# A smaller DMA scratch, and its SBUF given to more buffers in the mixers of a streaming encoder step

## The chip, the core and the metric

The kernel runs on one core of one Trainium2 chip. A core has five engines that run their own instruction queues in order and meet only at semaphores: TensorE (PE, matrix products, with its weight loads shown as PEld), VectorE (DVE), ScalarE (ACT), GpSimd (POOL) and SyncE (SP), which here only issues DMAs. ACT and POOL issue DMAs too. A DMA is issued in the order of the queue that it stands in, and an issue that has to wait holds back all that is behind it on that queue. On-chip memory (SBUF) has 128 partitions; a buffer takes some bytes of each. PE writes its results to another memory, PSUM, from which ACT and DVE fetch them.

The metric is the device time of one launch in microseconds (us), median of several runs. A profile is one execution, and its span runs from the first to the last instruction of the program.

## The reference

One layer of an encoder is applied to a prompt (2048 rows of 1024) and to a sample (8 requests of 16 rows) that shares the weights and brings a cache. Cut to what matters:

```python
h = rms_norm(x, norm_g[0])
z = h @ w_in                                   # columns: qa ka va | qb kb vb ob | ib fb
att = band_attention(qa, ka, va)               # 8 heads x 64, own chunk of 64 and 8 before, bias by distance
                                               # sample: 512 cached keys and values, and its own 16
hb, (c1, n1, m1) = mlstm_sequence(qh, kh, vh, ig, lf, c0, n0, m0)   # 4 heads x 128, a matrix state
mix = concat(rms_norm(att), sigmoid(ob) * head_norm(hb)) @ w_out
x = x + rms_norm(mix, norm_g[1])
u = rms_norm(x, norm_g[2]) @ w_up              # 1024 -> 5632
y = causal_conv_width_3(u)
x = x + rms_norm((gelu(gate) * up) @ w_down, norm_g[3])             # 2816 -> 1024
```

It returns the new rows, the keys and values to keep, the mLSTM's states, and the last rows of `u`. The sample's mLSTM starts from states that are inputs: for each of 4 heads and 8 requests a 128x128 matrix with a vector beside it (`state_c`, 129 columns).

## The kernel before, in words

All values are float32. A product is made of three products of "high" and "low" parts: each operand is split by ACT (a copy to a rounded type, the high part) and DVE (what is left, the low part), and `mm3` (lines 93 to 97) issues high*high, high*low, low*high. So every weight that comes from memory goes through a raw float32 tile, a split by ACT and DVE, and two tiles that PE reads.

The work up to about 1300 us, the mixers:

- *Projection.* The 17 tiles of 128 rows (16 of the prompt and the sample's one) are taken in two halves, `HALVES`. `norm_tile` (L209) loads a tile of x (`xr`), norms it and turns it on PE (`hT`). For each half 14 groups of columns of `w_in` are gone through, `GROUPS`: `va`, `qk`, `qb`, `vo`. `load_group` (L1158) brings a group's weights in two halves of 1056 columns at most through the tile `wraw` (the DMA at L1169, splits at L1175 and L1176). The results leave PSUM through a stage tile of two buffers (`st`), and go to DRAM by DMAs that ACT issues (L239, L275).
- *Attention.* `load_head` (L321) brings queries, keys and values of a head and a quarter of the prompt back from DRAM in raw tiles (`raw_tile`, L282), splits them (L342 to L356), and `att_unit` (L364) makes scores, weights and output. The bias depends on the distance alone: `build_bias` (L291) writes it to DRAM once for each head and row, eight broadcasts `relrow` (L302), from which `nb` is loaded (L325). `attention_sample` does the same for the sample, with keys and values of the cache in raw tiles (L847, L897).
- *mLSTM.* `prep_prompt` and `prep_sample` make the stabilisers; `mlstm` goes over pairs of blocks of 128 rows, with a result tile `num` of two buffers; `mlstm_sample` (L726) handles a head of the sample, and its `batches` takes two requests at a time: it loads their states into `cs` (L769), multiplies (L781, L782), updates the states in place (L785, L786) and stores them from there (L787). Before the change `cs` shares the two buffers of `num`.
- *Output projection.* `w_out_steps` (L929) brings `w_out` through `wraw` too; `project` (L962) makes the mix for one tile after another and writes the result to DRAM (`x2d`).

Two streams of units, attention and mLSTM, are interleaved with the projection by hand-written costs (`pump`, L171). That fixes the program's order. The tile framework then schedules it: it simulates the program on its own timeline and fixes each engine's order of instructions and each tile's buffer, waits included. So how many buffers a tile has changes where instructions stand on every engine. Priorities at a few places are pinned (`keep_in_program_order`).

From L1262 on comes the feed-forward part, in three blocks of rows: the up projection by a seven-product scheme (`product`, L1411), the convolution (L1428 on, with POOL's small copies), and the down projection (`down`). Its pools take the SBUF of the mixers' pools once those are closed (`open_ffn`, L1037). The only DMAs that POOL issues are 24 stores of finished rows in this part (L1378).

[...]

Of the kernel before, what the change touches and what calls it, by code (L numbers as in the profile page):

```python
# [10 lines left out]
F32 = mybir.dt.float32  # L11
# [6 lines left out]
P = 128  # L18
D = 1024
# [10 lines left out]
LS = 512 + DS  # L30
# [14 lines left out]
def hymba_step(ctx: ExitStack, tc: tile.TileContext, I: dict, O: dict):  # L45
    nc = tc.nc
# [13 lines left out]
    def ps_sm(name):  # L60
        return psum.tile([P, 512], F32, tag="sm", name=name)
# [25 lines left out]
    def norm_row(i):  # L87
        t = const.tile([P, D], F32, tag="grow", name=f"norm_row{i}")
        nc.sync.dma_start(t, I["norm_g"][i:i + 1, :].broadcast_to([P, D]))
        return t  # L90
# [35 lines left out]
    pr = p1.enter_context(tc.tile_pool(name="pr", bufs=1))  # L126
    pa = p1.enter_context(tc.tile_pool(name="pa", bufs=2))
    pm = p1.enter_context(tc.tile_pool(name="pm", bufs=2))
# [151 lines left out]
    relrow = dt_([HA, P, SQ], "relrow")  # L280

    def raw_tile(name):  # L282
        return pa.tile([P, LS], F32, tag="raw", name=name, bufs=3)

    rel = []

    def load_bias():
        rel.append(raw_tile("reln")[:HA, :SQ - 383])
        tc.keep_in_program_order(nc.sync.dma_start(rel[0], I["rel_rev"][:, 0:SQ - 383]))

    def build_bias():  # L291
        ext = dt_([HA, SQ], "ext")

        def unit():
            far, near = raw_tile("relf")[:HA, :383], rel[0]
            nc.vector.tensor_scalar(near, near, -1.0, None, op0=ALU.mult)
            nc.vector.tensor_copy(far, near[:, 0:1].broadcast_to([HA, 383]))
            nc.sync.dma_start(ext[:, 383:SQ], near)
            nc.sync.dma_start(ext[:, 0:383], far)
            yield 0.0, 0.75  # L300
            for h in range(HA):
                tc.keep_in_program_order(nc.sync.dma_start(relrow[h], ext[h:h + 1, :].broadcast_to([P, SQ])))  # L302
                yield 0.0, 0.0
                if h % 2:
                    yield 0.0, 0.0

        yield unit()
        yield FLUSH
# [12 lines left out]
    def load_head(s):  # L321
# [7 lines left out]
        s.nb = nbs[hh]  # L329
        rows = slice(hh * 64, hh * 64 + 64)  # L330
        qr = raw_tile(f"qraw{nm}")[:, :512]
        krs = [raw_tile(f"kraw{nm}_{g}")[:, :512] for g in s.segs]
        for r in range(2):
# [392 lines left out]
    def mlstm_sample(h):  # L726
        md, dec, cols = stab["s"]
        e = DH + 1
        nm = f"s{h}"
        col = lambda i: cols[:, i, h:h + 1]  # L730
        s = SimpleNamespace()
# [33 lines left out]
        def batches(bp):  # L765
            yield 0.0, 0.0
            bs = slice(2 * bp, 2 * bp + 2)
            cs = pm.tile([P, 2, e], F32, tag="num", name=f"cs{h}_{bp}", bufs=2)
            nc.sync.dma_start(cs, I["state_c"][h][:, bs])  # L769
            qz = pm.tile([P, 2, P], F32, tag="mqk", name=f"qz{h}_{bp}", bufs=2)  # L770
            nc.gpsimd.memset(qz, 0.0)
            for i in range(2):
                c = slice((2 * bp + i) * DS, (2 * bp + i + 1) * DS)
                nc.gpsimd.tensor_copy(qz[:, i, c], s.qt[:, c])
            vz = pm.tile([P, 2, e], F32, tag="mvo", name=f"vz{h}_{bp}", bufs=2)
            nc.vector.tensor_tensor(vz, s.va.unsqueeze(1).broadcast_to([P, 2, e]),
                                    ind[:, bs].unsqueeze(2).broadcast_to([P, 2, e]), op=ALU.mult)
            yield 0.0, 0.3
            cu = ps_sm(f"cu{nm}_{bp}")
            for i in range(2):  # L780
                nc.tensor.matmul(cu[:, 2 * e:3 * e], qz[:, i, :], cs[:, i, :], start=(i == 0), stop=(i == 1))  # L781
            nc.tensor.matmul(cu[:, :2 * e], s.kw, vz.rearrange("p b e -> p (b e)"), start=True, stop=True)  # L782
            nc.vector.scalar_tensor_tensor(s.num[:, 0, :], cu[:, 2 * e:3 * e], col(1), s.num[:, 0, :],
                                           op0=ALU.mult, op1=ALU.add)
            nc.vector.tensor_tensor(cs, cs, dec[:, h, bs].unsqueeze(2).broadcast_to([P, 2, e]), op=ALU.mult)  # L785
            nc.vector.tensor_tensor(cs, cs, cu[:, :2 * e].rearrange("p (b e) -> p b e", b=2), op=ALU.add)  # L786
            nc.sync.dma_start(O["c_sample"][h][:, bs], cs)  # L787
            yield 0.85, 0.8
# [11 lines left out]
        for bp in range(DB // 2):  # L800
            yield batches(bp)
# [127 lines left out]
    def w_out_steps():  # L929

        big = []
        g1.append(norm_row(1))
        late = wpool.tile([P, 2112], F32, tag="wl", name="wor67", bufs=2)
        nc.sync.dma_start(late[:, :2 * D], I["w_out"][:, 6 * D:])
        for k in range(KT):
            if k < 6:
                raw = pr.tile([P, 1056], F32, tag="wraw", name=f"wor{k}")[:, :D]
                nc.sync.dma_start(raw, I["w_out"][:, k * D:(k + 1) * D])
                if k == 0:
                    yield 0.0, 0.0  # L940
            else:
                raw = late[:, (k - 6) * D:(k - 5) * D]
            if k % 3 == 0:
                big.append(phT.tile([P, 6, D], F32R, tag="hT", name=f"wo{k}", bufs=3))
            h_, l_ = big[-1][:, k % 3 * 2, :], big[-1][:, k % 3 * 2 + 1, :]
            for c in (slice(0, 512), slice(512, D)):
                if k < 4:
                    nc.scalar.activation(h_[:, c], raw[:, c], AF.Copy, scale=gatt[:, k:k + 1])
                    nc.vector.scalar_tensor_tensor(l_[:, c], raw[:, c], gatt[:, k:k + 1], h_[:, c],
                                                   op0=ALU.mult, op1=ALU.subtract)  # L950
                else:
                    nc.scalar.copy(h_[:, c], raw[:, c])
                    nc.vector.tensor_tensor(l_[:, c], raw[:, c], h_[:, c], op=ALU.subtract)
                if k < 6:
                    yield 0.0, 0.6
            wo.append((h_, l_))
# [201 lines left out]
    def load_group(gi):  # L1158

        i = SRC[GROUPS[gi]]  # L1160
        src, n = (I["w_in0"], 2112) if i == 0 else (I["w_in1"][i - 1], 2048)
        h = wpool.tile([P, 2112], F32R, tag="wh", name=f"wi{i}_h{gi}", bufs=2)
        l = wpool.tile([P, 2112], F32R, tag="wl", name=f"wi{i}_l{gi}", bufs=2)

        def steps():
            q = n // 2
            for s in range(2):
                raw = pr.tile([P, 1056], F32, tag="wraw", name=f"wi{i}_raw{s}")
                nc.sync.dma_start(raw[:, :q], src[:, s * q:(s + 1) * q])  # L1169
                yield 0.0, 0.0  # L1170
                yield 0.0, 0.0
                for e in range(2):
                    c = slice(s * q + e * q // 2, s * q + (e + 1) * q // 2)
                    r = raw[:, e * q // 2:(e + 1) * q // 2]
                    nc.scalar.copy(h[:, c], r)  # L1175
                    nc.vector.tensor_tensor(l[:, c], r, h[:, c], op=ALU.subtract)  # L1176
                    yield 0.0, 0.6

        return h, l, steps()
# [21 lines left out]
    for n_, (half, gi) in enumerate(seq):  # L1201
        wh, wl, _ = pend
# [5 lines left out]
        i = int(g[2])  # L1208
# [15 lines left out]
        if n_ == len(seq) - 1:  # L1224
            out = project([0, 1, 2, 3, 4, 5, 6, 7, SAMPLE, 8, 9, 10, 11, 12, 13, 14, 15])
            split = w_out_steps()
            next(split)
            next(out)
# [174 lines left out]
    for b, tiles in enumerate(FBLOCKS):  # L1403
# [74 lines left out]
        for f in range(NF):  # L1478
# [7 lines left out]
            e, c = ec[:, 0:512], ec[:, 512:1024]  # L1486
# [208 lines left out]
```

## Time and profile before

| | |
|---|---|
| time, median of 3 runs | 2796.26 us (2793.03 to 2800.73) |
| span of the profiled execution | 2784.7 us |
| mean granted TensorE clock | 0.998 |
| busy in the span | PE 98%, weight loads 92%, DVE 67%, ACT 51%, POOL 16% |
| DMA | 486.05 MB, 175 GB/s over the span |

The profiled execution has no time of its own beside its span; the median of the runs lies 11.6 us above the span, for what stands before the first and after the last instruction.

How to read the lines shown below. A line of the windows gives a stretch in us from the span's start, its length, and the busy time and number of instructions of each engine in it. A line of the waits says which engine, at which tile and line, waited for whom: microseconds in all, times, and the longest. A line of the timeline gives a start, a duration, engine, line, operation and tile, and in brackets the idle time of the engine before it and what ended it; "SPq" and "ACTq" are DMA issues, which count as no busy time. Names stand without buffer numbers: `cus` is the product of the sample's state, `qk_st` the stage of a projected group.

### The profile page before, as it was taken

The page shows a single profiled execution, that of the slowest core. Times are in us where ns is not written, and L with a number is a line of the kernel's source. Part 1 is how long each engine was busy: PE and PEld are TensorE (multiplying, and loading weights), DVE is VectorE, ACT ScalarE, POOL GpSimd, SP SyncE. Part 2 cuts the span into 40 slices and gives each one's busy share as a digit, 9 for nine tenths or more (in the row PEclk, how much of TensorE's full clock was granted, in tenths as well). Part 3 has the DMA queues.
Part 4 walks back from the last instruction along what each step waited for, and adds up shares of the span by engine and source line. Part 5 has one row for each costly group of instructions (what it writes and reads, how often), then busy time and mean ns, then how long its engine had stood idle before and what let it go on. Part 6 is the DMA issues. An engine that isn't in the chain of part 4 may idle for free.

```text
span 2784.7 us, 47088 instructions
## 1 busy us (share of the span) xinstructions
PE 2723.8 (98%) x16587; PEld 2548.3 (92%) x16587; DVE 1876.3 (67%) x3447; ACT 1409.1 (51%) x2836; POOL 437.4 (16%) x895
## 2 busy tenths in 40 slices
PE   8999999999999999999999999999999999999998
PEld 7899999998899998888999988899999878999887
DVE  5344455656556668666999986457877864888855
ACT  4355555644356666544454555345455543555543
POOL 1000010212000003244111110011111310222220
PEclk9999999999999999999999999999999999999999
DMA  5544355557555555356655455644544774555585
GB/s 185 155 119 136 103 174 162 164 157 217 162 173 148 144 179 171 107 176 227 187 172 167 167 176 174 219 142 153 160 152 141 276 263 152 172 179 180 192 309 190
DMA packets 311883, 486.05 MB, mean 175 GB/s; under 512 B 55426, under 2 KB 150622, under 8 KB 311518
## 3 DMA queue, kind: packets, MB, share of 16 engines
q1 hardware_dynamic: 271134, 442.92, 50.1%
q10 hardware_dynamic: 38592, 33.83, 3.6%
q0 software_dynamic: 1920, 6.29, 0.6%
q8 instruction: 130, 2.13, 0.3%
q14 instruction: 107, 0.88, 0.1%
HBM read 359.36 MB, written 126.70 MB: 175 GB/s over the span
## 4 chain that ended last, share of the span: by engine, by line
PE 55%; DVE 2%; DMA 1%; issue 1%; ACT 1%; POOL 1%; SPq 0%; DVEq 0%; POOLq 0%; ACTq 0%
PE uec L95 6%; PE uec L96 6%; PE uec L97 6%; PE dn L97 4%; PE dn L96 4%; PE dn L95 4%; PE ua L97 3%; PE ua L95 3%; PE ua L96 3%; PE dnm L97 2%; PE dnm L95 2%; PE dnm L96 2%; PE wo L97 2%; PE wo L95 2%; PE wo L96 2%; PE ub L96 1%
## 5 line engine op out<-in xcount | busy, mean ns | idle before, releaser
L95 PE MATMUL uec<-B,wuh 128*128 128x384 f32 (+1 forms) x720 | 234.9, 328 | 2.2 <-DVE uu L1419 1.1
L96 PE MATMUL uec<-B,wuh 128*128 128x384 f32 (+1 forms) x720 | 235.1, 327 | 0.0
L97 PE MATMUL uec<-B,wul 128*128 128x384 f32 (+1 forms) x720 | 233.9, 327 | 0.0
L1266 DVE TENSOR_TENSOR gl<-gr,gh 128x768 fp32r<-128x768 f32 (+3 forms) x141 | 120.4, 863 | 145.8 <-ACT gh L1265 144.5
L1265 ACT CAST gh<-gr 128x768 fp32r<-128x768 f32 (+3 forms) x141 | 102.0, 735 | 200.1 <-PE dn L96 183.2
L1265 ACT CAST wuh<-wu 128x512 fp32r<-128x512 f32 x255 | 141.7, 617 | 112.1 <-PE uec L96 103.2
L95 PE MATMUL dn<-wdh,gh 128*128 128x512 f32 x466 | 182.4, 391 | 2.3 <-DVE ug L1419 2.3
L96 PE MATMUL dn<-wdl,gh 128*128 128x512 f32 x466 | 183.4, 394 | 0.0
L97 PE MATMUL dn<-wdh,gl 128*128 128x512 f32 x466 | 167.9, 396 | 0.0
L1266 DVE TENSOR_TENSOR wul<-wu,wuh 128x512 fp32r<-128x512 f32 x255 | 164.6, 683 | 2.8 <-DMA x2d<-mx 2.8
L393 DVE CUSTOM_DVE_ANT_0 tmp<-s,nb 128x640 f32<-128x640 f32 (+4 forms) x128 | 94.4, 737 | 96.6 <-PE s L383 94.8
L95 PE MATMUL vo<-wi_h,hT 128*128 128x256 f32 x544 | 155.1, 285 | 0.6 <-DVE mt L199 0.6
L97 PE MATMUL vo<-wi_h,hT 128*128 128x256 f32 x544 | 155.6, 286 | 0.0
L96 PE MATMUL vo<-wi_l,hT 128*128 128x256 f32 x544 | 154.8, 285 | 0.0
L95 PEld LDWEIGHTS uec<-B,wuh 128*128 128x128 f32 x720 | 135.0, 188 | 4.2 <-DVE uu L1419 1.6
L95 PE MATMUL qk<-hT,wi_h 128*128 128x384 f32 (+1 forms) x384 | 128.7, 335 | 7.4 <-ACT qk_st L224 6.6
L96 PEld LDWEIGHTS uec<-B,wuh 128*128 128x128 f32 x720 | 135.2, 188 | 0.2
L97 PEld LDWEIGHTS uec<-B,wul 128*128 128x128 f32 x720 | 135.1, 188 | 0.0
L406 DVE TENSOR_TENSOR ptl<-pt,pth 128x640 fp32r<-128x640 f32 (+4 forms) x128 | 93.6, 737 | 57.1 <-ACT pth L405 56.0
L394 ACT ACTIVATE tmp<-tmp,mn 128x640 f32<-128x640 f32 (+4 forms) x128 | 97.6, 762 | 64.6 <-DVE mn L393 61.9
L96 PE MATMUL qb<-hT,wi_h 128*128 128x384 f32 (+1 forms) x384 | 127.8, 333 | 0.0
L96 PE MATMUL qk<-hT,wi_h 128*128 128x384 f32 (+1 forms) x384 | 127.6, 332 | 0.0
(412 smaller groups left out, 8873.0 us busy)
## 6 DMA issues: line engine op xcount, KB each, us to landing
wu<-in_w_up SPq DMA_DIRECT2D x220, 256.0 KB, 4.1
wu<-wsd SPq DMA_DIRECT2D x176, 256.0 KB, 4.2
wdr<-in_w_down SPq DMA_DIRECT2D x132, 256.0 KB, 5.6
gr<-gd SPq DMA_DIRECT2D x78, 384.0 KB, 3.6
wi_raw<-in_w_in SPq DMA_DIRECT2D x52, 512.0 KB, 4.0
wsd<-ws SPq DMA_DIRECT2D x88, 256.0 KB, 2.8
gd<-g SPq DMA_DIRECT2D x44, 384.0 KB, 3.5
kraw<-kTd SPq DMA_DIRECT2D x112, 128.0 KB, 3.2
```

Of the source, the lines that this page charges most:

```text
L95: nc.tensor.matmul(out, ah, bh, start=start, stop=False, skip_group_check=onto)
L96: nc.tensor.matmul(out, ah, bl, start=False, stop=False, skip_group_check=onto)
L97: nc.tensor.matmul(out, al, bh, start=False, stop=stop, skip_group_check=onto)
L393: nc.vector.tensor_tensor_reduce(o_, s_, b_, 1.0, 3e38, ALU.add, ALU.min, accum_out=mn)
L394: nc.scalar.activation(tmp[:, :n], tmp[:, :n], AF.Exp, bias=mn, scale=-1.0, accum_out=rsum[:, i % 4, hh:hh + 1])
L406: nc.vector.tensor_tensor(s.ptl[:, sl, qc], ptv, s.pth[:, sl, qc], op=ALU.subtract)
L1265: nc.scalar.copy(h, r)
L1266: nc.vector.tensor_tensor(l, r, h, op=ALU.subtract)
```

## The change

The scratch for POOL's DMAs is built with 4,096 bytes of a partition in place of 16,384. Of the 12,288 bytes, 10,512 are given out: a second buffer of `wraw` (4,224 bytes), two more of the raw attention tiles (2 x 2,112), and two buffers of its own for the sample state `cs` (2 x 1,032). Nothing is computed in another way; the number of instructions that compute and of DMAs is the same.

```diff
     def raw_tile(name):
-        return pa.tile([P, LS], F32, tag="raw", name=name, bufs=3)
+        return pa.tile([P, LS], F32, tag="raw", name=name, bufs=5)
...
         def batches(bp):
             yield 0.0, 0.0
             bs = slice(2 * bp, 2 * bp + 2)
-            cs = pm.tile([P, 2, e], F32, tag="num", name=f"cs{h}_{bp}", bufs=2)
+            cs = pm.tile([P, 2, e], F32, tag="cs", name=f"cs{h}_{bp}", bufs=2)
...
-                raw = pr.tile([P, 1056], F32, tag="wraw", name=f"wor{k}")[:, :D]
+                raw = pr.tile([P, 1056], F32, tag="wraw", name=f"wor{k}", bufs=2)[:, :D]
...
-                raw = pr.tile([P, 1056], F32, tag="wraw", name=f"wi{i}_raw{s}")
+                raw = pr.tile([P, 1056], F32, tag="wraw", name=f"wi{i}_raw{s}", bufs=2)
...
-    nc = bacc.Bacc("TRN2", target_bir_lowering=False, num_devices=1)
+    nc = bacc.Bacc("TRN2", target_bir_lowering=False, num_devices=1, dynamic_dma_scratch_size=4096)
```

## The prediction

> **What bounds the kernel now.** I read the head of the page first, then busy time by stage, then what PE waited for.
>
> ```profile
> span 2784.7 us, 47088 instructions
> PE 2723.8 (98%) x16587; PEld 2548.3 (92%) x16587; DVE 1876.3 (67%) x3447; ACT 1409.1 (51%) x2836; POOL 437.4 (16%) x895
> ```
>
> PE is busy for 2723.8 of 2784.7 us. The change takes no matmul away, so only the 60.9 us in which PE stood idle can be won. Where they lie is told by the view of windows (columns after the length: busy PE, weight loads, DVE, ACT, POOL, clock, DMA share, GB/s):
>
> ```profile
> 0.00:150.00 150.00, 129.66 (x888) 124.99 (x889) 67.45 (x168) 63.39 (x133) 12.07 (x40) 0.99 0.54 165
> 150.00:500.00 350.00, 349.35 (x2480) 344.37 (x2479) 178.76 (x408) 181.42 (x425) 17.72 (x58) 1.00 0.46 138
> 500.00:750.00 250.00, 237.14 (x1676) 223.97 (x1675) 144.75 (x413) 117.27 (x303) 46.02 (x132) 1.00 0.59 179
> 750.00:1000.00 250.00, 249.81 (x1891) 246.25 (x1890) 148.93 (x338) 149.23 (x357) 15.58 (x47) 1.00 0.54 159
> 1000.00:1300.00 300.00, 293.24 (x1720) 252.86 (x1719) 217.01 (x364) 158.92 (x382) 98.49 (x139) 1.00 0.50 161
> 1300.00:2784.70 1484.70, 1464.64 (x7943) 1355.91 (x7941) 1119.42 (x1757) 738.86 (x1239) 247.48 (x479) 1.00 0.57 189
> ```
>
> Idle PE is 20.3 us in the start, 12.9 us between 500 and 750, 6.8 us between 1000 and 1300, and 20.1 us in the feed-forward part, half of that its tail. The mixers proper (150 to 500, 750 to 1000) lose under 1 us. The view of waits names what ended the idle time (us in all, times, longest):
>
> ```profile
> PE qk L95 <- ACT qk_st L224: 6.6, 2, 3.3
> PE cus L781 <- DMA cs<-in_state_c: 5.0, 6, 2.0
> PE va L95 <- ACT hT L198: 3.0, 2, 1.9
> PE cus L781 <- DVE nums L783: 1.2, 1, 1.2
> ```
>
> Two of these lines, `qk_st` and `cs`, touch the buffers of the change. The 5.0 us for `cs` do so openly. The 6.6 us for `qk_st` do so through SP's queue.
>
> **The feed-forward part.** The built order of the changed kernel is the same, instruction for instruction on every engine, from the middle of the output projection (about 1260 us) to the end. Its term is 0; what can move lies before 1300 us.
>
> **Second raw weight buffer.** Now each half of a weight group waits until the half before it has been split. SP pays for that, and whatever stands behind the load in its queue:
>
> ```profile
> SPq L1169 <- DVE lg_s_s L515: 18.0, 1, 18.0
> ```
> ```profile
> 58.10 0.33 SPq L1169 DMA_DIRECT2D wi_raw<-in_w_in  x1
> 58.53 2.51 SPq L302 DMA_DIRECT2D relrow<-ext  x4
> 66.18 0.88 SPq L325 DMA_DIRECT2D nb<-relrow  x2
> 67.58 2.20 SPq L302 DMA_DIRECT2D relrow<-ext  x2
> 69.88 0.75 SPq L334 DMA_DIRECT2D qraw<-qTd  x1
> 96.78 1.16 SPq L302 DMA_DIRECT2D relrow<-ext  x2
> ```
> ```profile
> 62.19 1.12 ACTq L239 DMA_DIRECT2D qTd<-qk_st  x2
> 81.98 0.62 ACT L342 CAST qs<-qraw 128x512 fp32r<-128x512 f32 x1 [10.99 <-DMA qraw<-qTd]
> 82.50 0.47 ACT L224 COPY qk_st<-qk 128x384 f32<-128x384 f32 x1
> 98.68 1.13 ACTq L239 DMA_DIRECT2D qTd<-qk_st  x2
> 108.02 0.48 ACT L224 COPY qk_st<-qk 128x384 f32<-128x384 f32 x1 [7.30 <-DMA qTd<-qk_st]
> ```
>
> Read it as a chain. The sixth weight load waits 18.0 us, until 58.10. Behind it stand the broadcasts that lay out the attention bias (`relrow`); four take from 58.53 to 66.18, 7.65 us, before the first use of their result is issued. The query load comes behind two more of them; ACT stands 10.99 us in `qs` until 81.98, and the eviction behind it comes at 82.50: PE's first 3.3 us. The last two broadcasts at 96.78 run beside the query store of 98.68, so the next eviction waits 7.30 us for its stage: the second 3.3 us.
>
> With two buffers the sixth load waits for the split of the fourth half alone. In the changed order that split stands on DVE right behind the third tile's low part, near 22 us by my estimate (the third load goes out at 18.27 us today, in a row below, and no longer waits for its forerunner). So the first four broadcasts leave near 22 us instead of 58.53, and only two stand before the first queries. At half of 7.65 us they are through some 4 us after their issue, the query store of 62.19 is no longer late, and I expect `qs` near 70 us, while the eviction behind it is needed when PE finishes two more chunks, near 74. The first wait goes: -3.3 us (bounds -3.3 and 0). The last two broadcasts still follow the second stabiliser load (`dec`) and still meet a query store, but a few microseconds earlier, when the stage buffers are less behind: between 0 and -3.3 us, I take -2.0. Next in line is the cast of the first keys on ACT, which I put just ahead of PE's need.
>
> At the very start both halves of the first group are now fetched at once:
>
> ```profile
> 10.70 0.33 SPq L1169 DMA_DIRECT2D wi_raw<-in_w_in  x1
> 18.27 0.36 SPq L1169 DMA_DIRECT2D wi_raw<-in_w_in  x1
> 18.72 6.05 SPq L212 DMA_DIRECT2D xr<-in_x_prompt  x2
> 36.39 0.33 SPq L212 DMA_DIRECT2D xr<-in_x_sample  x1
> ```
>
> The half of 10.70 us moves in front of the second tile of x. That lets the first tile's matmuls run through, but the second tile lands about 2 us later, and the eighth tile (the second of the two from 18.72) falls behind the early broadcasts and the first bias load. From 22 plus 7.65 us it would be issued near 30 and land near 34, 2 to 3 us before PE asks for it. Gain and loss are of one size; I take 0, with bounds from -3.0 (the whole wait of `va` on `hT`) to +3.3 (one stall such as PE now has).
>
> **The sample state's own buffers.** The row of 5.0 us counts six waits. In one head, SP's rows (the first pair elsewhere, undisturbed; the second disturbed) and PE's:
>
> ```profile
> 443.34 0.34 SPq L787 DMA_DIRECT2D out_c_sample<-cs  x1
> 445.70 0.33 SPq L769 DMA_DIRECT2D cs<-in_state_c  x1
> ...
> 562.45 0.35 SPq L1169 DMA_DIRECT2D wi_raw<-in_w_in  x1
> 563.13 0.34 SPq L787 DMA_DIRECT2D out_c_sample<-cs  x1
> 567.91 0.33 SPq L769 DMA_DIRECT2D cs<-in_state_c  x1
> ```
> ```profile
> 441.99 0.60 PE L782 MATMUL cus<-vz,kws 128*128 128x258 f32 x2
> ...
> 570.12 0.68 PE L781 MATMUL cus<-cs,qz 128*128 128x129 f32 x4 [0.44 <-DMA cs<-in_state_c]
> ```
>
> A batch pair's buffer comes free when its state has been stored: 441.99 to 443.34 (1.35 us) until the store is issued, 2.36 us to the next load, and 570.12 - 567.91 = 2.21 us until PE has the data, 5.9 us together. Where a weight load of 512 KB went out just ahead, 562.45, the middle part is 4.78 us. With buffers of their own the first two loads of each head no longer wait for the mLSTM's `num` to be stored; in the changed order they stand far ahead. The third and fourth still wait for their own store. There 44 to 62 matmuls lie between the last product of a pair and the first of the pair after next; at 250 us / 1676 of the window 500 to 750, 0.149 us each, that is 6.6 to 9.2 us against 5.9. And no weight load stands between the first stores and loads of a head any more. I take -4.0 of the 5.0 + 1.2 us; bounds -6.2 and 0.
>
> [...]
>
> **Two more raw attention buffers.** No wait of PE names `qraw`, `kraw`, `vraw`, `skr` or `svr`; SP stands for them, and PE's idle share of the mixers proper is under 1 us. Term 0; if the cover goes it costs what SP's other heads of queue cost (below).
>
> **Smaller scratch.** [...]
>
> ```profile
> q0 software_dynamic: 1920, 6.29, 0.6%
> out_y_prompt<-f POOLq DMA_DIRECT2D x24, 256.0 KB, 5.5
> ```
>
> 24 issues in the whole program, 80 packets each, two close together at most. Term 0; a blocked POOL could add at most one landing of 5.5 us per issue, on an engine that is busy 16%.
>
> **What the new order moves.** The build reorders nearly all mixer work. Between about 380 and 700 us the attention and mLSTM matmuls stand some 10 us of PE work earlier; near the end of the mixers they stand some 10 us later, so that the last head's work falls among the projection of tiles 7 and 16. There DVE is busy 217.01 of 300 us (72%): 10 us of moved work bring up to 7.2 us of DVE work to a stretch that PE may wait on. The number of PE instructions that have under 3 us of other PE work between their cause and themselves is much the same in both orders, though (46 before, 52 after). I take 0, bounds -3.0 and +7.2.
>
> **Sum.** -3.3 - 2.0 + 0 - 4.0 + 0 = -9.3 us. The profiled span becomes 2775.4 us. The runs' median, 2796.26 us, is 11.6 us above the span; that remainder stays, so 2796.26 - 9.3 = 2787.0 us. A step of 0.3% is 8.4 us, about what a measurement of this kernel tells from none (the three runs spread over 7.7 us).
>
> **Rivals.**
>
> *More than that goes.* With all bounds on the good side, -3.3 - 3.3 - 3.0 - 6.2 - 3.0 = -18.8: 2777 us. For it speaks that each stall shifts everything behind it; against it, that six steps must all come out well.
>
> *The waits only move.* The broadcasts cost their 7.65 us of DMA wherever they run. Brought forward to 22 us they meet the loads of the x tiles, in the one stretch where PE has nothing else to do, and the `cs` loads put ahead meet them too. Then about 3.3 us return at the start and the second `qk_st` wait stays (+2.0), and two of the `cs` waits stay (+2): -9.3 + 7.3 = -2, 2794 us. [...]
>
> *Slower: SP's head of queue.* The changed order puts a store of `cs` and the load that waits for it back to back, twice per head, ahead of the sample's keys and values and the mLSTM loads:
>
> ```profile
> SPq L769 <- DMA out_c_sample<-cs: 22.8, 7, 4.4
> ```
>
> SP already stands 22.8 us in seven such waits. If the four of the last two heads, beside the sample attention, each held PE up for the longest of them, 4.4 us, that is +17.6: -9.3 + 17.6 = +8.3, 2804.6 us. It decides from two such holds on (-9.3 + 8.8, no gain), and at four the kernel is slower; against it, five raw buffers let the keys run ahead.
>
> *The change does not do what it says.* The extra buffers are not taken up because the order is fixed elsewhere; 2796 us. Against it, the built order does differ.
>
> **How the numbers follow.** The forecast (-14 to -4 us, 2782 to 2792) has 0.50, of which 0.34 lies beyond 0.3%; the larger gain 0.10; waits only moved 0.20; SP's queue 0.15; nothing or a blocked POOL 0.05. Faster by over 0.3%: 0.34 + 0.10 = 0.44. Slower: 0.15 + 0.03 = 0.18. Within: 0.38. The range leaves out half of the larger gain and the worse part of the slower case: 2774 to 2806 us.
>
> **What would show it.** Right: four `relrow` issues before 35 us; no `qk <- qk_st` wait of 3 us near 80; `cs` waits of PE under 1.5 us in all; idle PE between 500 and 750 near 9 us; the feed-forward part as long as before to 1 us. Wrong: `hT_pt` or `va` waits grown by over 3 us before 50; new PE waits on `skh`, `svh` or `ms` between 500 and 750; over 10 us idle between 1000 and 1300; POOL waiting at its DMAs.

## The result and the profile after

The changed kernel takes 2806.94 us (median of 4, 2803.42 to 2808.86), the kernel before 2795.14 us beside it. The ratio is 1.0041, 95% interval 1.0029 to 1.0053: 11.8 us slower, where 2787.0 us and a gain of 9.3 us were forecast. 2806.94 us lies above the range too.

The head of the page and the stretches of the windows, as shown of before:

```profile
span 2801.7 us, 47030 instructions
PE 2730.9 (97%) x16587; PEld 2552.3 (91%) x16587; DVE 1868.5 (67%) x3447; ACT 1403.6 (50%) x2836; POOL 436.3 (16%) x895
```
```profile
0.00:150.00 150.00, 128.98 (x871) 123.20 (x872) 67.62 (x167) 61.32 (x131) 14.11 (x40) 0.99 0.56 174
150.00:500.00 350.00, 347.06 (x2452) 341.20 (x2451) 174.91 (x410) 176.63 (x422) 14.32 (x56) 1.00 0.46 138
500.00:750.00 250.00, 239.08 (x1707) 227.77 (x1706) 144.61 (x414) 119.74 (x308) 45.21 (x138) 1.00 0.60 179
750.00:1000.00 250.00, 248.53 (x1868) 244.52 (x1867) 141.57 (x324) 143.36 (x346) 11.42 (x39) 1.00 0.52 151
1000.00:1300.00 300.00, 282.88 (x1660) 243.72 (x1659) 205.06 (x365) 158.10 (x381) 90.70 (x132) 0.98 0.47 151
1300.00:2801.70 1501.70, 1484.35 (x8038) 1371.89 (x8037) 1134.70 (x1772) 744.43 (x1253) 260.57 (x491) 1.00 0.57 189
```

PE idles 70.8 us in place of 60.9. By stretch (length minus busy PE): 21.0 at the start (20.3 before), 2.9 (0.7), 10.9 (12.9), 1.5 (0.2), 17.1 (6.8), and 17.4 (20.1) in the feed-forward part. The one that stands out is 1000 to 1300 us, where the clock fell to 0.98 as well. Idle time is not all of it: of the 17.0 us by which the two spans differ, 9.9 are idle and 7.1 are PE's busy time, for the same 16587 products (the last section comes back to this). All of it lies ahead of the feed-forward part, whose first product starts 19.8 us later (1333.3 us, 1313.5 before). The waits of PE:

```profile
PE hT_pt L67 <- DVE xr L219: 10.7, 4, 8.2
PE mT_pt L67 <- DVE mr L985: 9.3, 4, 6.1
PE va L95 <- ACT hT L198: 4.9, 4, 1.9
...
PE cus L781 <- DMA cs<-in_state_c: 2.2, 2, 1.3
PE h2T_pt L1093 <- DVE t L1119: 2.1, 1, 2.1
...
PE va L95 <- ACT qk_st L224: 1.7, 1, 1.7
```

The waits that the forecast rested on did shrink: `cs` from 5.0 + 1.2 to 2.2 us, the two waits of 3.3 us on `qk_st` to 1.7 + 0.5. In their place stand waits that the kernel before did not have, above all `mT_pt` on `mr`, 9.3 us, in the output projection. The order of the work there belongs to a step that the prediction had priced at nothing, "what the new order moves".

**The start.** SP's queue, and the ACT row for the first query:

```profile
1.72 0.91 SPq L1169 DMA_DIRECT2D wi_raw<-in_w_in  x2
...
11.21 0.80 SPq L769 DMA_DIRECT2D cs<-in_state_c  x2
...
24.58 0.33 SPq L1169 DMA_DIRECT2D wi_raw<-in_w_in  x1
25.00 3.15 SPq L302 DMA_DIRECT2D relrow<-ext  x4
...
43.60 0.33 SPq L212 DMA_DIRECT2D xr<-in_x_sample  x1
```
```profile
74.65 0.62 ACT L342 CAST qs<-qraw 128x512 fp32r<-128x512 f32 x1 [4.43 <-DMA qraw<-qTd]
```

The broadcasts left at 25.00 us (58.53 before), `qs` came at 74.65 (81.98). But the sample's tile of x left at 43.60 in place of 36.39, and PE now stood at it (the 0.95 us are new; a wait of 1.10 us on `hT` stood at this place before too, at 48.05 us):

```profile
50.69 1.09 PE L67 MATMUL hT_pt<-ident,xr 128*128 128x128 f32 x8 [0.95 <-DVE xr L219]
52.89 0.39 PE L95 MATMUL va<-wi_h,hT 128*128 128x264 f32 x1 [1.10 <-ACT hT L198]
```

The wait of 3.3 us near 83 us is gone (one of 0.47 us stands at 91.61). The one near 108 us is gone as well, and the 1.7 us that are left come by another road:

```profile
103.56 1.16 SPq L302 DMA_DIRECT2D relrow<-ext  x2
```
```profile
106.98 0.48 ACT L224 COPY qk_st<-qk 128x384 f32<-128x384 f32 x1 [0.94 <-PE qk L97]
115.75 0.69 ACT L689 ACTIVATE w<-mb,colsp 128x128 f32<-128x128 f32 x2 [8.29 <-POOL mb L673]
```
```profile
116.86 0.39 PE L95 MATMUL va<-wi_h,hT 128*128 128x256 f32 x1 [1.71 <-ACT qk_st L224]
```

The last two broadcasts left at 103.56 us (96.78 before), and the eviction at 106.98 waited for PE alone, where it had stood 7.30 us for its stage. PE's 1.71 us come from an eviction at 116.35, ahead of which ACT stood 8.29 us for the mask `mb` of the mLSTM.

**The end of the mixers.** Rows of SP, POOL, DVE and PE around the longest new wait, with the landing of the bias load from the view of that tile:

```profile
1078.01 0.38 SPq L325 DMA_DIRECT2D nb<-relrow  x1
```
```profile
DMA to landing us min/median/max: 9.5/9.5/9.5
```
```profile
1082.44 0.41 POOL L673 TENSOR_SCALAR_AFFINE_SELECT mb<-mb 128x256 f32<-128x256 f32 x1 [6.70 <-DMA mb<-md]
1087.64 0.15 POOL L326 MEMSET nb<- 64x64 f32 x1 [4.79 <-DMA nb<-relrow]
...
1088.08 0.19 POOL L646 TENSOR_SCALAR ad<-ad 128x2 f32<-128x2 f32 x1
1088.36 0.71 POOL L647 TENSOR_TENSOR mf<-ad,nhalf 128x2 f32<-128x2 f32 x1
```
```profile
1089.10 0.62 DVE L653 SCALAR_TENSOR_TENSOR num<-num,mf,mvo 128x128 f32<-128x128 f32 x2 [6.50 <-POOL mf L647]
...
1096.58 0.47 DVE L985 TENSOR_SCALAR mr<-mr,att_rs 128x512 f32<-128x512 f32 x1
```
```profile
1097.11 1.12 PE L67 MATMUL mT_pt<-ident,mr 128*128 128x128 f32 x4 [6.13 <-DVE mr L985]
```

Read backwards: PE waits 6.13 us for `mr`; DVE comes to `mr` late, since it stood 6.50 us at POOL's `mf`; POOL had `mf` behind the fill that masks the last head's bias, and stood there 4.79 us for a load issued at 1078.01 and landed 9.5 us later. Before, the same load was issued at 1059.51 us, 12.6 us ahead of that `mf`:

```profile
1059.51 0.33 SPq L325 DMA_DIRECT2D nb<-relrow  x1
```
```profile
1064.16 0.14 POOL L326 MEMSET nb<- 64x64 f32 x1 [5.70 <-DMA nb<-relrow]
...
1072.15 0.71 POOL L647 TENSOR_TENSOR mf<-ad,nhalf 128x2 f32<-128x2 f32 x1
```

### The profile page after: what moved, and what is told of

The parts are those of the page before. It is cut to its first block, busy times and chain, and to the rows that moved or that the text cites. A ratio compares the mean times of both kernels' runs of the same rounds, so it can differ in the third digit from the quotient of the medians.

```text
span 2801.7 us, 47030 instructions
## 1 busy us (share of the span) xinstructions
PE 2730.9 (97%) x16587; PEld 2552.3 (91%) x16587; DVE 1868.5 (67%) x3447; ACT 1403.6 (50%) x2836; POOL 436.3 (16%) x895
## 4 chain that ended last, share of the span: by engine, by line
PE 50%; DVE 2%; DMA 2%; issue 1%; ACT 0%; POOL 0%; DVEq 0%; SPq 0%; POOLq 0%; ACTq 0%
PE uec L95 6%; PE uec L96 6%; PE uec L97 6%; PE dn L97 4%; PE dn L96 4%; PE dn L95 4%; PE ua L97 3%; PE ua L96 3%; PE ua L95 3%; PE dnm L97 2%; PE dnm L95 2%; PE dnm L96 2%; PE ub L96 1%; PE ub L97 1%; PE ub L95 1%
## 5 line engine op out<-in xcount | busy, mean ns | idle before, releaser
L97 PE MATMUL qk<-hT,wi_l 128*128 128x384 f32 (+1 forms) x384 | 127.9, 333 | 0.0
```

The costliest lines, as they stand in the source:

```text
L97: nc.tensor.matmul(out, al, bh, start=False, stop=stop, skip_group_check=onto)
```

## The experiments

Ratios are to the kernel before, timed on the same chip; that kernel's median was 2789 to 2795 us from chip to chip, so ratios are compared and not times. 0.0010 is 2.8 us. In brackets stand intervals of 95%.

**Holding the order fixed.** An instruction has the same name in nearly every build, whatever the buffers. So a build's order can be written down and imposed on another build, as a chain of dependencies without semaphores on each engine (in short):

```diff
     with tile.TileContext(nc, schedule_with_timeline_sim=True) as tc:
         hymba_step(tc, ins, outs)
+        pin_order(tc)
+def pin_order(tc):          # ORDER: a row of instruction names for each engine
+    ins = {i.name: i for i in tc.nc.cur_bb.bb.instructions}
+    for row in ORDER:
+        for last, this in zip(row, row[1:]):
+            tc.add_manual_dep(ins[this], last, NOSYNC, reason="pinned order")
```

**Buffers or order.** The changed kernel in the order of the kernel before.

```diff
-ORDER: none, the scheduler's own
+ORDER: the rows of the kernel before
```

> The buffers and the scratch of the changed kernel, but every engine's instructions pinned to the order in which they stand in the kernel before. Theory A (the loss comes from the new order of instructions, not from the buffers): no wait of mT_pt on mr above 2 us between 1030 and 1200 us, the waits for cs and for qk_st no longer than before, the time 2786 to 2797 us, at or below the kernel before. Theory B (more loads under way at once collide on the DMA engines, in whatever order): slower than before by 6 us or more, 2801 to 2810 us, with longer landings than before and new waits of PE on loaded tiles.

Measured: 2786.81 us, ratio 0.9963 (0.9951 to 0.9975). The instructions and DMA issues of every engine stand in its trace in the same order as in that of the kernel before, and the new idle time is gone:

```profile
1000.00:1300.00 300.00, 293.08 (x1707) 252.28 (x1707) 213.54 (x361) 158.40 (x380) 99.54 (x138) 0.99 0.50 158
```

Theory A holds, theory B falls. The buffers alone win 10 us by the ratio (8.2 us by the medians); the order that the scheduler made for them loses about 20 us. (The mirror, the new order with the old buffers, was not run: the 20 us are the price of the new order with all the buffers in place.)

**One wait in the new order.** The two fills of `nb` moved on POOL behind `att_rs`, nothing else; POOL's row by what its instructions write:

```diff
   wssq1_0, mb3_10,
-  nb7_2, nb7_2,
   ad2_12, mf2_12, mvo3_8, n1_1_ms, n1_1_rs, att3_ms, att3_rs,
+  nb7_2, nb7_2,
   mx1
```

> The changed kernel with its order pinned, but for two instructions: on POOL the two fills that mask the last head's bias (nb, L326 and L327) stand behind att_rs of the fourth tile of the output projection instead of ahead of ad and mf of the third head's third pair. Theory A1 (the largest single loss is POOL's queue: the fills wait for a bias load that lands at 1087.5 us, and mf, num, the normalisation of mx and mr stand behind them): the 6.3 us wait of mT_pt on mr near 1090 us falls below 2 us, the dip of the granted clock behind it (0.90 in 1075 to 1100) goes too, and the time is 2795 to 2801 us, 6 to 12 below the changed kernel. Theory A2 (the place is short of slack all round; another wait takes over at once): less than 3 us are won, 2804 to 2808 us.

Measured: 2805.61 us, 1.0034 (1.0021 to 1.0047), where the changed kernel has 1.0041; the two cannot be told apart. The chain was read rightly, its price was not. Of this kernel's waits:

```profile
PE mT_pt L67 <- DVE mr L985: 5.7, 4, 2.6
```

The wait of 6.13 us is one of 1.58 us now, yet the other three tiles wait 4.2 us in all where they had 3.2, and idle PE between 1000 and 1300 us is 15.2 us in place of 17.1. Theory A2: the place is short of slack all round.

**Parts alone, in the scheduler's own order.**

```diff
-            cs = pm.tile([P, 2, e], F32, tag="num", name=f"cs{h}_{bp}", bufs=2)
+            cs = pm.tile([P, 2, e], F32, tag="cs", name=f"cs{h}_{bp}", bufs=2)
```

> Only the sample state's own two buffers, with the smaller scratch; everything else as before, the order left to the scheduler (it moves far less than in the full change). Theory A: the cs waits of PE fall from 5.0 us to under 2.5 us, no new late stall, 2790 to 2796 us. The prediction's own term for this part was -4.0 us, 2792 us. Theory B: at most 1 us is won, 2795 to 2799 us.

Measured: 1.0004 (0.9995 to 1.0012). Nothing is won; PE still waits 5.4 us for `cs`. Theory B.

```diff
-                raw = pr.tile([P, 1056], F32, tag="wraw", name=f"wi{i}_raw{s}")
+                raw = pr.tile([P, 1056], F32, tag="wraw", name=f"wi{i}_raw{s}", bufs=2)
```

(and the same in `w_out_steps`)

> Only the second raw weight buffer, with the smaller scratch; the order left to the scheduler, which moves nearly all mixer work. The prediction's own terms for this part: the two waits of 3.3 us of qk on qk_st gone or halved, -5.3 us, 2791 us. Theory A: those waits go, but the new order brings stalls of its own, at the start or late in the mixers, that are not there in the kernel before: 2793 to 2806 us. Theory B: the start alone gets longer, by 3 to 6 us before 60 us, and the late mixers stay as before.

Measured: 2820.57 us, 1.0097 (1.0084 to 1.0110): 27 us slower, outside every expectation. Idle PE is 24.1 us in the first 300 us (20.3 before), 18.9 between 300 and 800 (13.7), 13.4 between 1000 and 1300 (6.8).

**Parts alone, in the old order.** Here only the waits can change. ORDER is that of the kernel before; the edits are the two above, one each, and for the attention

```diff
-        return pa.tile([P, LS], F32, tag="raw", name=name, bufs=3)
+        return pa.tile([P, LS], F32, tag="raw", name=name, bufs=5)
```

> Only the second raw weight buffer (and the smaller scratch), with every engine pinned to the order of the kernel before. Two buffer changes that take part in the 8.2 us won by all three under the old order are thus told apart. The prediction's term for this part was -3.3 - 2.0 = -5.3 us, 2790 us (2787 to 2793). The rival: in the old order the loads stand where they stood, behind other waits of SP, so that the 18.0 us wait on SP turns into another one and nothing is won: 2793 to 2797 us.

> Only the sample state's own two buffers (and the smaller scratch), with every engine pinned to the order of the kernel before. The prediction's term for this part was -4.0 us, 2791 us (2789 to 2793), with the cs waits of PE under 1.5 us. The rival: the third and fourth load of each head still wait for their own store, so that at most the two first loads of each head gain, -1 to -2 us, 2793 to 2795 us.

> Only the two more raw attention buffers (and the smaller scratch), with every engine pinned to the order of the kernel before. The second raw weight buffer alone won 0.4 us there and the sample state's own buffers 0.7 us, all three together 8.2 us. Theory R (the raw attention buffers, which the prediction priced at 0, are what pays: SP stood 49.4 us at the values' loads L351 and 36.7 us at the keys' L337 in the kernel before): 2786 to 2790 us. Theory P (SP needs both, since with one buffer more the next load in its queue waits for the other kind): 2792 to 2796 us.

Measured: 0.9998 (0.9988 to 1.0009), 0.9999 (0.9990 to 1.0009), 1.0000 (0.9991 to 1.0009). No part wins anything alone that is clear of 3 us. These three also show that the pinning itself costs nothing that can be measured. With the weight buffer alone one of the two waits on `qk_st` goes (3.6 us are left of 6.6), and PE's waits of `va` on `hT`, for tiles of x, grow from 3.0 to 5.9 us. The waits of SP and PE between 300 and 800 us suggest what keeps the rest. With the weight buffer alone:

```profile
SPq L847 <- DVE svl L902: 18.1, 9, 6.4
SPq L351 <- DVE kl L347: 14.2, 3, 11.8
...
PE cus L781 <- DMA cs<-in_state_c: 5.2, 5, 2.2
```

With the raw attention buffers alone:

```profile
SPq L1169 <- DVE wi_l L1176: 22.0, 11, 5.0
...
SPq L1169 <- DMA wi_raw<-in_w_in: 11.5, 6, 3.2
...
PE cus L781 <- DMA cs<-in_state_c: 5.1, 5, 1.8
```

SP stands at whichever kind of load is still short, and the `cs` loads stand behind it in the queue. Added over all rows of the five load lines (L337, L351, L847, L897, L1169), SP's waits in this stretch are 129.5 us before, 96.6 with the weight buffer, 73.3 with the attention buffers, 35.9 with all three groups. That sum is no price, though: the changed kernel in its own order has 151.4 us of it, and PE waits only 2.2 us for `cs` there.

**Pairs in the old order, and all three again.**

> The second raw weight buffer and the two more raw attention buffers, without the sample state's own, in the order of the kernel before. Theory P2 (SP needs both kinds: with one alone it stands at the other, 22.0 + 11.5 us at the weights L1169 between 300 and 800 us with more attention buffers alone, 18.1 + 14.2 + 10.0 us at L847, L351 and L897 with the weight buffer alone): ratio to the kernel before 0.996 to 0.998, most of the 0.9963 of all three. Theory P3 (all three are needed): 0.9985 to 1.000.

> The second raw weight buffer and the sample state's own buffers, without the raw attention buffers, in the order of the kernel before. Theories P2 and P3 both: SP still stands at the raw attention buffers, the cs waits of PE stay near 5 us, ratio 0.999 to 1.001. A ratio below 0.998 would speak against both.

> The two more raw attention buffers and the sample state's own, without the second weight buffer, in the order of the kernel before. Theories P2 and P3 both: SP still stands at the weight buffer (L1169), ratio 0.999 to 1.001. A ratio below 0.998 would speak against both, and for the sample state's loads standing behind the attention loads alone.

> All three groups in the order of the kernel before once more, on the chip of the three pairs. If the gain found at first (0.9963) is the kernel's and not that chip's: 0.995 to 0.9975, with the cs waits of PE at 2 to 3.5 us. If it was the draw of a few executions: 0.998 to 1.000.

Measured: weights and attention 0.9982 (0.9973 to 0.9991), weights and state 0.9994 (0.9985 to 1.0002), attention and state 0.9986 (0.9976 to 0.9996), all three 0.9975 (0.9966 to 0.9985). The gain of all three is confirmed. The pairs with the attention buffers win 4 to 5 us, the pair without them nothing that is clear of 1. Neither theory is settled: 0.9982 lies between the ranges of P2 and P3, neither had a place for the 3.9 us of attention and state, and the intervals of the pairs overlap. What is shown is that each group alone wins nothing and the three together 7 to 10 us. Where on PE these lie is not shown: idle PE is 62.5 and 58.6 us in the two profiles of all three, 60.9 in that of the kernel before, which was one of its quick executions.

**Where the new order loses.** The order of one build up to a product of PE, then what is left in the order of the other; always with all buffers.

```diff
+new_early_old_late: changed up to PE's 6670th product, then before
+old_early_new_late: before up to PE's 6670th product, then changed
+new_to_800:         changed up to PE's 5472nd product, then before
+new_start_only:     changed up to PE's 1796th product, then before
```

> The buffers of the changed kernel. The order of the changed kernel up to the last product of qb (about 1002 us), from there on what is left in the order of the kernel before. Theory L (the new order loses late, where the last heads run beside the output projection): 2787 to 2794 us, and idle PE between 1000 and 1300 us back below 10 us from 17.1. Theory E (the loss of 20 us against the old order is spread over the mixers): 2796 to 2802 us.

> The mirror of the run before it: the buffers of the changed kernel, the order of the kernel before up to the last product of qb (about 1002 us), from there on what is left in the order of the changed kernel. Theory L: 2799 to 2806 us, with idle PE between 1000 and 1300 us above 13 us. Theory E: 2792 to 2797 us.

Measured: 2803.48 us, 1.0032 (1.0019 to 1.0045), and 2798.29 us, 1.0012 (1.0001 to 1.0023). The first lies above both theories' ranges, the second between them. Against the old order throughout (0.9963, and 0.9975 on another chip), the late part alone costs 10 to 14 us. The early part seems to cost 16 to 19, but the cut itself makes two waits there:

```profile
1010.28 0.41 PE L382 MATMUL s<-kh,qs 128*128 128x320 f32 x1 [3.17 <-DVE ptl L406]
1014.38 0.58 PE L418 MATMUL ot<-pth,vhl 128*128 128x256 f32 x1 [3.26 <-ACT pth L405]
```

So the cut was put where both orders have done the same work (about 800 us), and another at 270 us.

> The buffers of the changed kernel. The order of the changed kernel up to PE's 5472nd product (about 800 us), from there on the order of the kernel before. At that place both orders have done the same work, so no seam is cut; the lag of the attention and mLSTM work, which in the new order grows to 61 products between 920 and 1020 us, is gone. Theory L2 (the lag costs the 12 us that PE loses more between 1000 and 1300 us): 2793 to 2797 us, idle PE in 1000 to 1300 us below 10 us. Theory E2 (what is lost is lost before 800 us): 2800 to 2806 us.

> The buffers of the changed kernel. The order of the changed kernel for the start alone, up to PE's 1796th product (about 270 us), then the order of the kernel before. In the profiles the new order loses 5 us more before 100 us (late tiles of x: hT_pt, va) and 2.4 us less between 100 and 200 us (the wait of qk on qk_st). If that is all that the start does, the time is 2.5 us above the run with the old order throughout: 2788 to 2791 us. If the first loads collide more than one profile shows: 2792 to 2797 us. If the start is a gain, as the prediction had it (-5.3 us): 2780 to 2784 us.

Measured: 0.9991 (0.9983 to 1.0000) and 0.9975 (0.9964 to 0.9986); on a kernel before of 2795 us, the base of the expectations, that is 2792 us, just below theory L2's range, and 2788 us, where the start costs what the profiles show. Between 1000 and 1300 us, the changed order from about 1002 us on, and the old order from about 800 us on:

```profile
1000.00:1300.00 300.00, 284.54 (x1657) 243.92 (x1656) 205.83 (x357) 157.10 (x377) 91.73 (x133) 0.99 0.47 150
```
```profile
1000.00:1300.00 300.00, 294.37 (x1720) 253.86 (x1719) 215.76 (x362) 159.30 (x383) 97.97 (x138) 0.99 0.49 159
```

Idle PE is 15.5 us in the one and 5.6 us in the other. The steps: all buffers in the old order 0.9963 and 0.9975 (two chips); the new start adds 0 to 0.0012, the stretch to 800 us 0.0016 on the same chip, the rest 0.0050, to 1.0041. In us: -7 to -10, then 0 to +3, +4.5, +14, each step known to some 4 us by the intervals. By the other cut the late part is 10 to 14 us, so the two agree.

**Is it the lag?** In the built orders the attention and mLSTM work falls behind the projections between 920 and 1020 us: 312 of the output projection's 816 products stand ahead of the last score product before, 356 in the changed kernel. The next run turns that around by hand, and two more take builds whose own order stands elsewhere.

```diff
+mixers_earlier: all buffers, before's order, but from PE's 6138th product on each instruction of attention and mLSTM up to 75 places earlier
+raw_cs_own_order: bufs=5 for raw, cs with its own two; the scheduler's order
+wraw_raw_own_order: bufs=5 for raw, bufs=2 for wraw; the scheduler's order
```

> The buffers of the changed kernel in the order of the kernel before, but from PE's 6138th product (about 905 us) on the attention and mLSTM instructions of every engine stand up to 75 places earlier against the projections, so that 13 to 28 products of theirs more are done at the same point of the projection. It turns the suspected lag around. If the lag has a price per product (12 us for about 50), this wins 2 to 5 us on the old order: 2782 to 2785 us, the fastest so far. If the old order already has enough slack there: 2785 to 2789 us; if a new place of waits is cut where the shift begins: 2790 to 2796 us.

> The two more raw attention buffers and the sample state's own, without the second weight buffer, in the scheduler's own order for them (335 products of the projection ahead of the last score product). Theory G (the late loss grows with that lag, 14 us for 44 products): some 7 us lost between 1000 and 1300 us, idle PE there 11 to 15 us, ratio to the kernel before 1.000 to 1.003. Theory N (the lag says nothing, each order has its own stalls): idle PE there anywhere between 6 and 20 us.

> The second raw weight buffer and the two more raw attention buffers, without the sample state's own, in the scheduler's own order for them, which is that of the changed kernel but for few places (356 products ahead, as there). Theory G: as the changed kernel, ratio 1.003 to 1.006, idle PE between 1000 and 1300 us 14 to 19 us, with the wait of mT_pt on mr near 1090 us. If the sample state's buffers in the new order were the cause: 0.998 to 1.001.

Measured: 2808.20 us, 1.0062 (1.0050 to 1.0075), slower than every expectation for it; 1.0012 (1.0004 to 1.0021) and 1.0057 (1.0045 to 1.0069), both as theory G has it. Idle PE between 1000 and 1300 us by the number of products ahead:

| order | products ahead | idle PE, us |
|---|---|---|
| before, and eleven runs with that late order | 312 | 5.6 to 7.9 |
| new order up to 1002 us, then the old one, with the two waits at the cut | 312 | 12.7 |
| attention and state, own order | 335 | 11.5 |
| changed kernel, fill moved, new late part, weights and attention in own order | 356 | 15.2 to 17.1 |
| weights alone, own order | 384 | 13.4 |
| shifted by hand | 308 | 25.1 |

Among the orders that the scheduler made, the loss grows from 312 to 335 to 356; the same stalls come back whichever buffers are there (without the state's own buffers too), so those are not the cause. (In that order they do their work: without them PE waits 5.4 + 0.8 us for `cs`, with them 2.2, and the ratio is 1.0057 against 1.0041, not clear of the intervals.) But the hand-shifted order has the smallest count and the greatest loss, and 384 loses less there than 356. The lag is a sign of the loss in this kernel, not shown to be its cause. What is shown: in this stretch every late order other than the old one lost 5 to 18 us more, through waits of PE above all on `mr`, `mt`, `mx` and `t`. Which link would have to move first stays open.

## Why the prediction was wrong, point by point

- *What the new order moves: 0, bounds -3.0 and +7.2.* **This step failed.** It is 18 to 22 us: 0 to 3 at the start, 4.5 from there to 800 us, 14 after it. The prediction named the place (the last head among the projection, DVE at 72%) and then dismissed it, because the number of PE instructions with little cover was much the same over the whole program (46 and 52). A count over the whole program does not say where they stand; idle PE between 1000 and 1300 us went from 6.8 to 17.1 us. The bound was DVE's share of 10 us of moved work, but the longest delay came by a chain through four queues, SP, POOL, DVE and PE, and DVE itself stood idle in it for 6.5 us. That chain is not the whole price: without it the time is the same within the intervals. Which links make up the 14 us stays open.
- *Second weight buffer, first `qk_st` wait: -3.3.* The mechanism came as told: four `relrow` at 25.00 us (22 estimated), `qs` at 74.65 (70 estimated), no wait of 3 us near 80. The gain was given back where the rival "the waits only move" had put it, at the tiles of x (`va` on `hT` 3.0 to 5.9 us with the weight buffer alone in the old order): with all buffers in place the new start is 0 to 3 us slower than the old one, so the step at the very start, taken as 0 with bounds -3.0 and +3.3, came out on its bad side.
- *Second `qk_st` wait: -2.0.* It went, but not as told: the last two broadcasts came 7 us later and not a few us earlier, and the eviction beside them no longer waited for its stage. The 1.7 us that PE still waits on `qk_st` there come from ACT standing at `mb`.
- *The sample state's own buffers: -4.0.* In the changed kernel's trace 6.2 us became 2.2: that size, in one execution each. But the reason given left something out: the loads stand behind others in SP's queue. Alone, in the old order, SP stood 18.5 us at L1169 for `wi_l` and 15.5 us at L847 for `svl` between 300 and 800 us, the 5.0 us stayed 5.0 and the time was 0.9999.
- *Raw attention buffers: 0.* Alone that is what they are worth (1.0000). But "no wait of PE names them" was no ground for setting them aside in the set: under the old order the two pairs that have them win 4 to 5 us, and the pair without them nothing that is clear of 1. The intervals overlap, so their share is indicated and not settled.
- *Smaller scratch: 0.* No run changes the scratch alone, and none shows which DMAs use it, so none shows this term by itself. It was in every run of the old order, the three at 1.000 among them, so it costs nothing there that can be measured. POOL's 24 stores took 0.56 to 0.76 us each to issue in the kernel before and in the changed one, and landed after 5.5 and 5.6 us (medians); no wait of POOL in front of one was longer than 0.3 us.
- *The feed-forward part: 0.* From its first product to the end it takes 1468.5 us against 1471.3 before, and 1468.6 to 1476.3 in one execution each of the other runs, all with the same order of PE's products there. Nothing speaks against the term.
- *Rival, SP's head of queue.* The stores and loads of `cs` did stand back to back (SP's waits there rose from 22.8 to 33.5 us), but PE's waits for `cs` fell. Slower came by another road.
- *The base.* The prediction put the 11.6 us between the span and the median down to work outside the span. The execution of the changed kernel with a span of 2801.7 us took 2803.42 us: that remainder is 1.7 us. The profiled execution of before, about 2786.4 us by that, was simply 9 us quicker than the median, so the same goes for the 11.6 us in the account of the time before.
- *The signs to watch.* The one that decided had been listed: "over 10 us idle between 1000 and 1300", and it was 17.1. Of the signs of being right the four `relrow` before 35 us and the missing wait near 80 came; `cs` stayed at 2.2 us (under 1.5 was asked) and idle PE between 500 and 750 at 10.9 (near 9).

The sum is 2787.0 us, and the buffers in the old order took 2786.8 and 2787.5 us. That is no success of the terms: singly they measured 0, and only together 7 to 10 us.

## What to carry to other kernels

Where a scheduler orders the program by its own timeline, a buffer count is two changes, the waits and the order; price them apart, and measure them apart by pinning the old order. Here that keeps the gain (0.9963 and 0.9975, the best ratios of this study) and drops a loss of twice its size. Here, buffers whose loads stand on one DMA queue, SP's, paid only as a set: each part alone measured nothing, so try the set before dropping a part. That SP stood at whichever load was still short fits this, and is not shown to be the reason. Before a forecast, compare the two orders where slack is least, not over the whole program.

## What the hardware showed unexpectedly

PE's longest new wait cost more than its length. Behind the 6.13 us of idle time the same product ran 0.47 us in place of 0.31, and the starts lay 0.27 us apart in place of 0.14. First the changed kernel, then the kernel before:

```profile
1098.56 0.47 PE L382 MATMUL s<-kh,qs 128*128 128x320 f32 x1
1098.83 0.47 PE L383 MATMUL s<-kl,qs 128*128 128x320 f32 x1
```
```profile
1076.09 0.31 PE L382 MATMUL s<-kh,qs 128*128 128x320 f32 x1
1076.23 0.31 PE L383 MATMUL s<-kl,qs 128*128 128x320 f32 x1
```

And the granted clock (the third number from the end) of the changed kernel in that stretch and the one after it, then in shorter ones:

```profile
1075.00:1100.00 25.00, 18.75 (x100) 15.86 (x99) 14.84 (x32) 10.63 (x32) 6.85 (x12) 0.90 0.57 168
1100.00:1125.00 25.00, 24.45 (x144) 21.23 (x143) 18.79 (x38) 15.51 (x38) 6.92 (x11) 0.96 0.47 138
```
```profile
1096.00:1097.00 1.00, 0.00 (x0) 0.00 (x0) 1.00 (x3) 0.04 (x1) 0.38 (x1) 0.50 0.00 0
1100.00:1102.00 2.00, 2.00 (x12) 2.00 (x10) 1.97 (x8) 2.00 (x6) 0.58 (x3) 0.50 0.09 27
1102.00:1104.00 2.00, 2.00 (x16) 1.82 (x15) 1.91 (x7) 1.90 (x6) 0.51 (x1) 1.00 0.67 231
```

The clock stood at 0.50 while PE still waited and was back at 1.00 from 1102 us on. From 1097.11 us on that makes 4.9 us at half the clock: by an estimate 2.4 us lost on top of the 6.13. The slow products begin behind the wait, at 1097.11 us, and end near 1101.9. In the kernel before, without such a wait there, the granted clock is 1.00 in both stretches of 25 us. In the run with the two fills moved, where no wait of PE on `mr` is above 2.6 us, it is 0.99 between 1000 and 1300 us, against 0.98 in the changed kernel and 1.00 before. From what length on a wait brings the clock down is not shown.

So idle time alone undercounts what the new order cost here. With the weight buffer alone in its own order the span is 33.9 us longer than before, 15.2 us of it idle and 18.7 us longer busy time for the same products; the granted clock over its span is 0.992, 0.998 before and 0.996 in the changed kernel.

The executions of one program differ by more than the effects at stake. The kernel before took 2783.8 to 2800.7 us on the chips of this study, with one and the same order, so one profile tells where time can be lost, and not to 5 us how much. Part of this spread goes with the granted clock: of the 116 executions timed beside the experiments, the 17 with 0.998 or more took 2.8 us less than the median of their chip on the mean, the 9 with 0.995 or less 3.1 us more.
